# Thirteen tiles of a dense expert table read during a key search, into a buffer of later activations

## The chip, the cores and the metric

The kernel runs on one core of a Trainium2 chip. The core has five engines that this text speaks of: PE (matrix multiplies), DVE (elementwise work and the max/index searches), ACT (activations, casts, evacuation of results), POOL (some elementwise work, and the issue of indirect gathers) and SP (which issues the plain loads and stores). Each works through its own queue in order, and they wait for each other on semaphores. Sixteen DMA engines move data between the main memory and the on-chip memory.

The metric is device time in microseconds. Before the change three runs took 1619.58 to 1623.15 us, with a median of 1620.98 us. A separate execution under the profiler gives the views that this text quotes.

## What is computed

The reference is one hybrid decoder block on 512 tokens of width 1024: three attention branches (a forgetting attention, a sliding window, a cross attention into a memory) are gated, merged and added to `x`, and then comes a product-key expert layer, which is the part that the change touches:

```python
q = (h @ w_q).reshape(B, S, PEER_HEADS, 2, half)
s1 = einsum('bshd,hkd->bshk', q[..., 0, :], keys1)
s2 = einsum('bshd,hkd->bshk', q[..., 1, :], keys2)
v1, i1 = lax.top_k(s1, PEER_TOPK);  v2, i2 = lax.top_k(s2, PEER_TOPK)
cand = (v1[..., :, None] + v2[..., None, :]).reshape(..., PEER_TOPK * PEER_TOPK)
sv, si = lax.top_k(cand, PEER_TOPK)
experts = i1[si // PEER_TOPK] * N_KEYS + i2[si % PEER_TOPK]
gates = softmax(sv)
a = einsum('cd,ced->ce', h, u[experts])
out = einsum('ce,ced->cd', gelu(a) * gates, v[experts])
```

There are 8 heads, 16 chosen experts for each head and token, and 16384 experts, so `u` and `v` are tables of 16384 rows of 1024 floats (64 MiB each).

## The kernel before

The 512 tokens are four blocks of 128. Block 0 goes first through the mixers and its own key search; blocks 1 to 3 follow as one group. For the expert layer the blocks are treated in two ways. Blocks 0 and 1 are gathered: for each of their 128 chosen experts per token a row of `u` and later a row of `v` is fetched by an indirect DMA that POOL issues (L833), and DVE (L843, L852), or ACT and POOL (L848, L849), work it in. Blocks 2 and 3 (`DENSE`) are dense: their activations against all 16384 experts are computed by PE, 128 tiles of 128 experts each, and the gates, which are zero for an expert that wasn't chosen, are multiplied in. A **U tile** is such a tile of the table, transposed on the host (`uT`), 128 x 1024 floats or 512 KB. `dense_u(k)` reads tile k, multiplies it with the dense tokens `h2f` (L971, eight multiplies, which the trace counts as sixteen matmuls) and puts the GELU of the result into `ga(k)` (L973), which is slot k of the tile `soon`. `soon` has 52 slots of 256 floats for each partition; the slots from 52 on are in a tile that is opened later.

The stages around the change, in the order of the program:

- **The second search** (`search(qq, h2T, f, BIG)`, for blocks 1 to 3). For each head SP loads two halves of the query weights `w_pq` into a ring of three buffers `raw` (`load_raw`, L110), ACT rounds them into `whi` (L116), DVE subtracts to get `wlo` (L128), PE multiplies three times (L142 to L144) with the tokens, which stand in the wide tiles `hhi` and `hlo`, ACT copies the result into `qp` (L716), PE makes the scores (L720), ACT copies them into `s` (L723), and DVE finds the sixteen best of each (L678 to L682). The search is a generator which yields an estimated cost after each piece; their running sum is `spent`, about 105 at the end. The loop around it starts a gathered row of block 0 with every 4.6 of cost (`step(apart=True)`: POOL issues the gather, ACT scales the row, POOL adds it), and calls `dense_u` for U tiles 0 to 7 whenever `spent` has passed another 13. Those eight tiles are read by `load_raw`, that is into the same ring of three `raw` buffers as the query weights.
- **The cover stage.** U tiles 8 to 31 go through PE while DVE weighs the gates (`weigh`), works out the chosen experts (`choose`, `numbers_of`) and adds rows of `v` for block 0. From tile 8 on a U tile is read into a ring of six (`URING`), three in `hhi` and three in `hlo`, as soon as the tile six before it is used up; `fetch_u_to` asks for five tiles ahead. `hhi` and `hlo` come free when the search has made its last query product.
- **The spread stage.** DVE builds one-hot sides (L1026), PE multiplies them into gates (L1041), DVE weighs the kept activations (L1044), and U tiles 32 to 56 (`LAG` is 57) go through PE in between.
- **The last stage.** All 128 tiles of `v` go through PE, with the 71 U tiles that are left, whose ring is now the three places of `hhi`.

Up to the end of the search the order of every engine's instructions is worked out by a planner that simulates the program with estimated times; `keep_in_program_order` pins one instruction behind the one that the program issued before it on the same engine. After the search (`tc.manual_schedule`) the orders of PE, DVE and POOL are those of the program, and the planner orders only SP and ACT.

Of the kernel before, what the change touches and what calls it, by code (L numbers as in the profile page):

```python
# [16 lines left out]
S, D, NB, KC = 512, 1024, 4, 8  # L17
# [4 lines left out]
NK = 128  # L22
# [5 lines left out]
ND = len(DENSE)  # L28
TD = 128 * ND
FIRST_U, COVER, DURING, AFTER = 8, 24, 25, 0  # L30
KEPT = FIRST_U + COVER
SPILT = (128 - KEPT) // 3
AMONG, UNWEIGHED = 1.0, 14
LAG = FIRST_U + COVER + DURING + AFTER
GA_LATE = 6
URING, URING_V = 6, 3
# [20 lines left out]
def tile_block(ctx: ExitStack, tc: tile.TileContext, t: dict, out: bass.AP):  # L57
    nc = tc.nc
# [12 lines left out]
    def bank(tag):  # L71
        return psum.tile([128, 512], F32, tag=tag, name=tag, bufs=BANKS[tag])
# [26 lines left out]
    def load_raw(src, n):  # L99
        loads[0] += 1  # L100
        pool = early[0] if early and loads[0] % (RAW_MORE + 3) >= 3 else wp
        raw = pool.tile([128, WSLOT], F32, tag="raw", name="raw")
        fill(raw, src, n)
        return raw

    def fill(raw, src, n):
        if len(src.shape) == 3:
            nc.sync.dma_start(raw[:, :n].rearrange("p (c w) -> p c w", c=src.shape[0]), src.rearrange("c p w -> p c w"))
        else:
            nc.sync.dma_start(raw[:, :n], src)  # L110
# [29 lines left out]
    def mm3(ps, l, r, first=True, last=True):  # L140
        (lh, ll), (rh, rl) = l, r
        PE.matmul(ps, lh, rh, start=first, stop=False)  # L142
        PE.matmul(ps, lh, rl, start=False, stop=False)  # L143
        PE.matmul(ps, ll, rh, start=False, stop=last)  # L144
# [4 lines left out]
    def wide(tag, nb, dt=F32):  # L149

        slot = big.tile([128, (1 if tag == "mg0" else BIG) * D], dt, tag=tag, name=tag)
        return slot[:, :nb * D]

    def by_token(x):
        return x.rearrange("p (b d) -> p b d", d=D)
# [44 lines left out]
    def factors(sums, nb):  # L200

        ss = small_f(BIG, "rss", 2)[:, :nb]
        V.reduce_sum(ss, sums[:, :nb], axis=AX.X)
        return rsqrt_mean(ss, nb, D)

    def diagonals(r, nb):
        dg = small.tile([128, BIG, 128], F32, tag="dg", name="dg", bufs=1)
        for b in range(nb):
            A.activation(dg[:, b], ident, AF.Copy, scale=r[:, b:b + 1])
        return dg  # L210

    def turn(xs, g, hi, lo, dg=None, tags=("tp", "sc")):

        w = 128 * len(xs)
        for dc in range(KC):
            ps = bank(tags[dc % len(tags)])
            for b, x in enumerate(xs):
                dst, src = ps[:, b * 128:(b + 1) * 128], x[:, dc * 128:(dc + 1) * 128]
                if dg is None:
                    PE.transpose(dst, src, ident)  # L220
                else:
                    PE.matmul(dst, src, dg[:, b], start=True, stop=True)
            A.activation(hi[dc], ps[:, :w], AF.Copy, scale=g[:, dc:dc + 1])
            if lo:
                V.scalar_tensor_tensor(lo[dc], ps[:, :w], g[:, dc:dc + 1], hi[dc].bitcast(F32),
                                       op0=OP.mult, op1=OP.subtract)
# [692 lines left out]
    gq, acc, late, v_raw, u_raw = {}, {}, [], {}, {}  # L919
    soon = dp.tile([128, LAG + 1 - GA_LATE, TD], F32, name="ga", bufs=1)  # L920

    def ga(k):
        s = k % (LAG + 1)
        return soon[:, s] if s <= LAG - GA_LATE else late[0][:, s - (LAG + 1 - GA_LATE)]

    def fetch_u(k):
        if not FIRST_U <= k < NK:
            return
        s = (k - FIRST_U) % URING if k < LAG else (k - LAG + 1) % URING_V
        if s % BIG == 0:  # L930
            if k - FIRST_U < URING:
                u_ring[s // BIG] = by_token(wide(("hhi", "hlo")[s // BIG], BIG))
        u_raw[k] = u_ring[s // BIG][:, s % BIG]
        if k > LAG + 2:
            tc.keep_in_program_order(nc.scalar.dma_start(u_raw[k], t["uT"][k]))
        else:
            nc.sync.dma_start(u_raw[k], t["uT"][k])

    u_ring, u_next = [None, None], [FIRST_U]

    def fetch_u_to(k):
        while u_next[0] <= min(k, NK - 1):
            fetch_u(u_next[0])
            u_next[0] += 1

    def split_u(k):
        return k >= LAG and (k - LAG) % U_SPLIT > 0

    def dense_u(k):

        if k < FIRST_U:
            w = load_raw(t["uT"][k], D)[:, :D]
        else:
            fetch_u_to(min(k + URING - 1, LAG + 1) if k < LAG else k)
            w = u_raw.pop(k)
        if split_u(k):
            hi, lo = (gp[0].tile([128, D], F32R, tag=tag, name=tag, bufs=1) for tag in ("uhi", "ulo"))
            A.copy(hi, w)
            yield
            V.tensor_sub(lo, w, hi.bitcast(F32))  # L960
            yield
            ps, hi, lo = bank("mm"), *(x.rearrange("p (n w) -> p n w", n=KC) for x in (hi, lo))
            for dc in range(KC):
                mm3(ps[:, :TD], (hi[:, dc], lo[:, dc]), [x[dc] for x in h2s], dc == 0, dc == KC - 1)
            A.activation(ga(k), ps[:, :TD], AF.Gelu)
            return
        w = w.rearrange("p (n w) -> p n w", n=KC)
        yield
        ps = bank("mm")
        for dc in range(KC):  # L970
            PE.matmul(ps[:, :TD], w[:, dc], h2f[dc], start=dc == 0, stop=dc == KC - 1)  # L971
            yield
        A.activation(ga(k), ps[:, :TD], AF.Gelu)  # L973
# [5 lines left out]
    with tc.tile_pool(name="qb", bufs=2) as qq:  # L979
        turn([x1[b] for b in GROUPS[1]], g2, *h2T)  # L980
        spent, dg, credit[0] = 0.0, None, 0.0
        for cost in search(qq, h2T, f, BIG):
            spent += cost
            if dg is None and spent > 12.0:
                V.tensor_copy(rstd[:, 1:NB], factors(sums, BIG))
                dg = diagonals(rstd[:, 2:NB], ND)
                turn([x1[b] for b in DENSE], g2, h2f, None, dg)
            credit[0] += cost
            while credit[0] >= PER_ROW and NJ <= done[0] < known[0]:
                credit[0] -= PER_ROW  # L990
                with tc.high_priority(-LATER):
                    step(apart=True)
            if k_u < FIRST_U and spent > 104.0 / FIRST_U * (k_u + 1):
                list(dense_u(k_u))
                k_u += 1
# [36 lines left out]
    def spread(n):  # L1032
# [9 lines left out]
        c = t0 % TG  # L1042
        kept = soon[:, :KEPT, i * 128 + t0:i * 128 + t0 + GT]
        V.tensor_mul(kept, ps[:, :, :KEPT].rearrange("p t k -> p k t"), kept)  # L1044
        for hf in range(3):
            k0 = KEPT + hf * SPILT
            A.copy(stage[0][hf][:, :, c:c + GT], ps[:, :, k0:k0 + SPILT].rearrange("p t k -> p k t"))
        if c + GT == TG:
            for hf in range(3):
                k0 = KEPT + hf * SPILT  # L1050
                nc.sync.dma_start(gd[i][:, k0 // GK:(k0 + SPILT) // GK, t0 // TG],
                                  stage[0][hf].rearrange("p (a k) t -> p a (k t)", k=GK))

    def get_gates(k, part):

        k -= k % GK
        if not KEPT <= k < NK or not 0 <= part < GQ_PARTS:
            return
# [52 lines left out]
    while k_u < FIRST_U + COVER:  # L1111
        if k_u == FIRST_U + UNWEIGHED:
            list(weigh(cp, f, 1))
        list(dense_u(k_u))
        k_u += 1
# [19 lines left out]
    for n in range(AHD, NBAT + AHD):  # L1135
        if n < NBAT:
            build_sides(n)
        if n == NBAT - PLAIN_ROWS:
            ahead[0] = AHEAD
        if n == NBAT - V_EARLY:  # L1140
            for k in range(VFAR):
                fetch_v(k)
        credit[0] += STEPS_N
        while credit[0] >= 1.0 and done[0] < known[0]:
            credit[0] -= 1.0
            step()
        if (n + 4) % PER == 0 and n + 4 < NBAT:
            turn_block((n + 4) // PER)
        spread(n - AHD)
        for _ in range(STEPS_U):  # L1150
            if tile_u is None and FIRST_U + COVER + n * DURING // NBAT >= k_u:
                tile_u = dense_u(k_u)
                next(tile_u)
                k_u += 1
            elif tile_u is not None and next(tile_u, 1):
                tile_u = None
# [132 lines left out]
```

## Time and profile before

| | |
|---|---|
| median of three runs | 1620.98 us |
| profiled execution | 1613.45 us, of which its span from first to last instruction is 1611.6 us |
| DVE busy in the span | 1406.2 us (87%) |
| ACT busy, POOL busy | 782.9 us (49%), 780.6 us (48%) |
| first matmul of a U tile | 689.6 us from the start of the span |
| first matmul of U tile 8 | 771 us |
| first one-hot side of the spread stage | 857.4 us |
| moved by the DMA engines | 531.85 MB, mean 330 GB/s |

Times inside the profile are microseconds from the start of the span. In a timeline a row is a start, a duration, the engine, the line of the kernel and the operation, then what is written and read; several alike are merged (x16), and square brackets give the idle time of the engine before the row and what ended it. In the list of waits a row says who waited for whom, and the three numbers are the total in microseconds, the number of times, and the longest. In the windows table every engine has its busy time in the window, then come the granted TensorE clock, the mean share of the DMA engines that were busy, and GB/s. Busy times of merged rows can overlap by a little, since an instruction may start before the one before it has fully ended.

### The profile page before, as it was taken

What the parts mean: (1) busy time and instruction counts of PE and PEld (TensorE: products, weight loads), DVE (VectorE), ACT (ScalarE), POOL (GpSimd) and SP (SyncE); (2) the same over time, 40 slices, a digit from 0 to 9 for tenths busy, and PEclk for the clock granted to TensorE, in tenths of its full rate; (3) what the DMA queues carried; (4) which work ended last, traced back from release to release, by engine and by line L of the source; (5) the groups of instructions that cost most, each with busy time, mean ns of one, the idle gap of its engine ahead of it and who ended that gap; (6) DMA issues with size and microseconds to landing.
All of it is one profiled execution on the core that took longest, in us unless ns stands there. A gap on an engine that the chain in (4) does not pass through costs nothing.

```text
span 1611.6 us, 26380 instructions
## 1 busy us (share of the span) xinstructions
PE 1532.9 (95%) x9030; PEld 1377.0 (85%) x9030; DVE 1406.2 (87%) x2721; ACT 782.9 (49%) x1782; POOL 780.6 (48%) x625
## 2 busy tenths in 40 slices
PE   5999999998998999998999999899999999999998
PEld 5999899988887989987888999688888888888887
DVE  5677458889888999999999999889899999999997
ACT  6787437645445443553116888344344343433432
POOL 1100011767566455588664333556655566555551
PEclk9999999999998999999999999999999999999999
DMA  8586753899998899967898999999999999999995
GB/s 300 176 283 223 236 196 118 285 358 310 326 344 287 280 360 342 326 203 264 320 404 304 367 385 350 379 394 394 399 409 407 395 411 408 410 412 409 406 407 215
DMA packets 180406, 531.85 MB, mean 330 GB/s; under 512 B 17456, under 2 KB 46384, under 8 KB 180272
## 3 DMA queue, kind: packets, MB, share of 16 engines
q0 software_dynamic: 73728, 268.47, 44.6%
q1 hardware_dynamic: 96752, 226.04, 38.6%
q10 hardware_dynamic: 9792, 35.66, 5.6%
q8 instruction: 71, 1.16, 0.3%
q14 instruction: 63, 0.52, 0.1%
HBM read 515.42 MB, written 14.68 MB: 329 GB/s over the span
## 4 chain that ended last, share of the span: by engine, by line
PE 36%; DVE 22%; DMA 17%; issue 15%; POOL 7%; ACT 2%; SPq 0%; DVEq 0%; POOLq 0%; ACTq 0%
DMA row<-in_peer_u_dram,eidx 8%; DMA row<-in_peer_v_dram,eidx 7%; POOL row L833 6%; PE mm L143 6%; PE mm L144 6%; PE mm L142 6%; DVE mg L852 6%; DVE o L1026 3%; DVE scr L843 3%; PE mm L971 3%; DVE wlo L128 2%; PE mm L295 2%; PE sc L142 1%; PE sc L143 1%; PE sc L144 1%
## 5 line engine op out<-in xcount | busy, mean ns | idle before, releaser
L833 POOL DMA_INDIRECT row<-in_peer_v_dram,eidx x256 | 346.0, 1351 | 269.2 <-DVE mg L852 150.0
L833 POOL DMA_INDIRECT row<-in_peer_u_dram,eidx x256 | 330.9, 1292 | 271.6 <-DVE scr L843 161.8
L843 DVE SCALAR_TENSOR_TENSOR scr<-row,own 128x1024 bf16<-128x1024 f32 x256 | 314.5, 1228 | 31.7 <-DMA row<-in_peer_u_dram,eidx 29.6
L128 DVE TENSOR_TENSOR wlo<-raw,whi 128x1024 fp32r<-128x1024 f32 (+1 forms) x243 | 305.6, 1259 | 36.3 <-ACT whi L116 35.7
L852 DVE SCALAR_TENSOR_TENSOR mg<-row,acts,mg 128x1024 f32<-128x1024 f32 x237 | 304.4, 1285 | 20.5 <-DMA row<-in_peer_v_dram,eidx 18.2
L971 PE MATMUL mm<-h2f,hhi 128*128 128x256 f32 x976 | 223.2, 379 | 1.6 <-ACT ga L973 1.6
L971 PEld LDWEIGHTS mm<-h2f,hhi 128*128 128x128 f32 x976 | 182.5, 190 | 26.6 <-ACT ga L973 2.0
L116 ACT CAST whi<-raw 128x1024 fp32r<-128x1024 f32 (+1 forms) x148 | 155.0, 1050 | 90.2 <-PE mm L143 47.1
L189 POOL TENSOR_TENSOR rsy<-rsv,mhalf 128x4 f32<-128x4 f32 (+5 forms) x25 | 38.8, 1553 | 219.8 <-DVE rsv L188 126.3
L1089 ACT CAST ah<-ga 128x256 fp32r<-128x256 f32 x116 | 47.0, 407 | 150.8 <-PE tp L143 118.1
L1091 ACT CAST whi<-raw 128x1024 fp32r<-128x1024 f32 x96 | 100.4, 1046 | 39.6 <-PE tp L144 26.0
L142 PE MATMUL mm<-hhi,whi 128*128 128x384 f32 x320 | 110.8, 347 | 5.9 <-ACT ga L973 4.6
L143 PE MATMUL mm<-hlo,whi 128*128 128x384 f32 x320 | 111.2, 347 | 0.0
L144 PE MATMUL mm<-hhi,wlo 128*128 128x384 f32 x320 | 110.1, 344 | 0.0
L142 PE MATMUL mm<-whi,hhi 128*128 128x256 f32 (+1 forms) x360 | 104.6, 292 | 3.0 <-DVE g L572 1.9
L142 PE MATMUL sc<-whi,ah 128*128 128x512 f32 x256 | 107.3, 419 | 0.0
L143 PE MATMUL sc<-wlo,ah 128*128 128x512 f32 x256 | 101.1, 395 | 3.4 <-DVE wlo L128 3.4
L143 PE MATMUL mm<-wlo,hhi 128*128 128x256 f32 (+1 forms) x360 | 103.1, 287 | 0.2 <-DVE wlo L128 0.2
L144 PE MATMUL mm<-whi,hlo 128*128 128x256 f32 (+1 forms) x360 | 101.7, 284 | 0.0
L973 ACT ACTIVATE ga<-mm 128x256 f32<-128x256 f32 x84 | 31.7, 379 | 143.5 <-PE mm L971 143.4
L144 PE MATMUL sc<-whi,al 128*128 128x512 f32 x256 | 101.1, 395 | 0.0
L142 PE MATMUL tp<-whi,ah 128*128 128x512 f32 x256 | 100.6, 393 | 0.0
(289 smaller groups left out, 3941.8 us busy)
## 6 DMA issues: line engine op xcount, KB each, us to landing
raw<-in_peer_v_dram SPq DMA_DIRECT2D x96, 512.0 KB, 8.1
hhi<-in_uT_dram ACTq DMA_DIRECT2D x68, 512.0 KB, 7.7
raw<-in_w_tr_dram SPq DMA_DIRECT2D x48, 512.0 KB, 5.0
raw<-in_w_nat_dram SPq DMA_DIRECT2D x40, 512.0 KB, 5.7
last<-in_peer_v_dram SPq DMA_DIRECT2D x32, 512.0 KB, 7.4
hhi<-in_uT_dram SPq DMA_DIRECT2D x28, 512.0 KB, 6.7
raw<-in_w_o_dram SPq DMA_DIRECT2D x24, 512.0 KB, 6.1
hlo<-in_uT_dram SPq DMA_DIRECT2D x24, 512.0 KB, 7.2
```

Of the source, the lines that this page charges most:

```text
L116: A.copy(hi[:, :n * w], raw[:, :n * w])
L128: V.tensor_sub(lo, raw, hi.bitcast(F32))
L142: PE.matmul(ps, lh, rh, start=first, stop=False)
L143: PE.matmul(ps, lh, rl, start=False, stop=False)
L144: PE.matmul(ps, ll, rh, start=False, stop=last)
L833: G.indirect_dma_start(out=r, out_offset=None, in_=t["peer_" + tab], in_offset=bass.IndirectOffsetOnAxis(ap=eidx[b][:, j:j + 1], axis=0))
L843: V.scalar_tensor_tensor(scr, r, 1.0, h2n[b], op0=OP.mult, op1=OP.mult, accum_out=acts[b][:, c]))
L852: V.scalar_tensor_tensor(x1[b], r, acts[b][:, c], x1[b], op0=OP.mult, op1=OP.add))
L971: PE.matmul(ps[:, :TD], w[:, dc], h2f[dc], start=dc == 0, stop=dc == KC - 1)
L1026: V.tensor_tensor(o, numbers[:, None, None, :].to_broadcast([128, 2, GT, NK]), eT[:, :2, ts, None].to_broadcast([128, 2, GT, NK]), op=OP.i ...
L1089: A.copy(ah, a)
L1091: A.copy(hi, raw)
```

## The change

U tiles 0 to 12 (`PRE_U`) are read into `soon`: tile k goes into slots 4k to 4k+3, which have its size, so 13 tiles fill the 52 slots. The activation of a tile is written to slot k when that tile has been multiplied, and slot k belongs to tile k // 4, which has been used by then. The reads are issued by SP in the loop around the second search, tile k as soon as `spent` is over 6 k, each pinned behind the SP instruction that the program issued before it. Tiles 0 to 7 no longer use `load_raw`. `dense_u` is called at the same places as before; for tiles 0 to 7 it asks for no reads. The ring in `hhi` and `hlo` begins with tile 13, which together with 14 to 18 is asked for at `dense_u(8)`. The place of a tile in the ring is counted from 13 on, and the last tile that is asked for in the spread stage is 57, where it was 58.

```diff
+PRE_U = 13
...
     def fetch_u(k):
-        if not FIRST_U <= k < NK:
+        if k < PRE_U:
+            u_raw[k] = soon[:, 4 * k:4 * k + 4].rearrange("p a b -> p (a b)")
+            tc.keep_in_program_order(nc.sync.dma_start(u_raw[k], t["uT"][k]))
             return
-        s = (k - FIRST_U) % URING if k < LAG else (k - LAG + 1) % URING_V
+        s = (k - PRE_U) % URING if k < LAG else (k - LAG + 1 + (LAG - 1 - PRE_U) % URING) % URING_V
         if s % BIG == 0:
-            if k - FIRST_U < URING:
+            if k - PRE_U < URING:
                 u_ring[s // BIG] = by_token(wide(("hhi", "hlo")[s // BIG], BIG))
         u_raw[k] = u_ring[s // BIG][:, s % BIG]
...
-    u_ring, u_next = [None, None], [FIRST_U]
+    u_ring, u_next = [None, None], [0]
...
     def dense_u(k):
 
-        if k < FIRST_U:
-            w = load_raw(t["uT"][k], D)[:, :D]
-        else:
-            fetch_u_to(min(k + URING - 1, LAG + 1) if k < LAG else k)
-            w = u_raw.pop(k)
+        if k >= FIRST_U:
+            fetch_u_to(min(max(k, PRE_U) + URING - 1, LAG) if k < LAG else k)
+        w = u_raw.pop(k)
...
+            while u_next[0] < PRE_U and spent > 6.0 * u_next[0]:
+                fetch_u_to(u_next[0])
             credit[0] += cost
```

## The prediction, on record before the result

> **What bounds the kernel now.** I read the table of windows first, one window for each stage, then the waits and the timelines of the two stages that the change touches.
>
> ```profile
> span 1611.6 us, 26380 instructions
> ...
> core 0: us, PE busy (x) PEld busy (x) DVE busy (x) ACT busy (x) POOL busy (x), PEclk, DMA share, GB/s
> 645.00:690.00 45.00, 43.53 (x263) 42.72 (x262) 44.61 (x112) 22.27 (x38) 25.00 (x25) 0.96 0.88 315
> 690.00:735.00 45.00, 40.34 (x224) 38.21 (x224) 44.91 (x253) 23.51 (x34) 34.44 (x32) 0.96 0.64 212
> 735.00:771.00 36.00, 31.55 (x166) 28.20 (x166) 33.15 (x250) 10.64 (x18) 33.16 (x31) 1.00 0.73 261
> 771.00:856.00 85.00, 83.36 (x387) 73.05 (x386) 80.69 (x131) 12.64 (x29) 50.49 (x39) 1.00 0.97 374
> 856.00:1000.00 144.00, 141.35 (x897) 131.01 (x896) 143.81 (x202) 120.15 (x468) 48.78 (x48) 1.00 0.99 352
> ...
> 1040.00:1594.00 554.00, 542.91 (x2771) 465.35 (x2770) 509.14 (x672) 218.16 (x337) 314.79 (x213) 1.00 1.02 402
> ```
>
> The search (the first three windows) is DVE's: in 126 us it is idle for 0.39 + 0.09 + 2.85 = 3.3 us, while PE is idle for 10.6 us. The cover stage (771 to 856) is a tie: PE idles 1.6 of 85 us, DVE 4.3. The spread stage is DVE's (0.2 us idle of 144). Only in the last stage are the DMA engines full (1.02, 402 GB/s) with PE next to them (98%).
>
> So the question is what a U tile that comes earlier can do for DVE in the search, and whether PE's tie in the cover stage is worth anything. The search's small idle times are seen in the timelines of DVE, ACT and PE:
>
> ```profile
> 750.61 0.68 DVE L678 MAX8 v<-s 128x8 f32<-128x128 f32 x3 [1.24 <-ACT s L723]
> ...
> 760.00 0.68 DVE L678 MAX8 v<-s 128x8 f32<-128x128 f32 x3 [1.57 <-ACT s L723]
> ...
> 729.07 1.05 ACT L116 CAST whi<-raw 128x1024 fp32r<-128x1024 f32 x1 [4.23 <-DMA raw<-in_w_pq_dram]
> ...
> 758.07 1.15 ACT L848 ACTIVATE row<-row,acts 128x1024 f32<-128x1024 f32 x1 [4.79 <-DMA row<-in_peer_v_dram,eidx]
> ...
> 759.49 0.48 ACT L723 COPY s<-sc 128x384 f32<-128x384 f32 x1
> ...
> 754.10 3.62 PE L971 MATMUL mm<-h2f,raw 128*128 128x256 f32 x16
> 759.64 0.94 PE L720 MATMUL sc<-keys,qp 128*128 128x128 f32 x6 [1.92 <-ACT qp L716]
> 760.41 7.07 PE L971 MATMUL mm<-h2f,raw 128*128 128x256 f32 x32
> 767.68 3.69 PE L971 MATMUL mm<-h2f,raw 128*128 128x256 f32 x16 [0.19 <-DMA raw<-in_uT_dram]
> 771.21 3.62 PE L971 MATMUL mm<-h2f,hhi 128*128 128x256 f32 x16
> ```
>
> DVE stalls twice, 1.24 and 1.57 us, for the copied scores of the last heads. The second copy stands in ACT's queue behind a row of `v` for which ACT had waited 4.79 us. No U tile holds PE up but the last, by 0.19 us, and then PE goes from tile 7 straight on to tile 8 at 771.21. There is no gap at the end of the search that an earlier read could close, since the ring's first reads had been issued 19 us before:
>
> ```profile
> 752.40 0.33 SPq L937 DMA_DIRECT2D hlo<-in_uT_dram  x1
> 752.78 1.68 SPq L937 DMA_DIRECT2D hhi<-in_uT_dram  x3
> ```
>
> Then the end of the cover stage, DVE and PE:
>
> ```profile
> 854.87 2.59 DVE L852 SCALAR_TENSOR_TENSOR mg<-row,acts,mg 128x1024 f32<-128x1024 f32 x2
> 857.38 4.61 DVE L1026 TENSOR_TENSOR o<-tg,eT 128x1024 f32<-128x1024 f32 x4
> ...
> 856.00 0.38 PE L1013 MATMUL acc<-cst,e 128*128 128x128 f32 x2
> 859.13 1.32 PE L1041 MATMUL sc<-o 128*128 128x128 f32 x8 [2.65 <-issue]
> ```
>
> DVE goes from the last rows (until 857.46) to the one-hot sides without a gap. PE is through with tile 31 at about 856 and then stands still for 2.65 us until the first sides are there. A PE that comes earlier to this point waits longer.
>
> **The change part by part.**
>
> *Reads of tiles 0 to 12.* SP issues 13 loads in the search where it issued 8, and six ring loads at its end as before (now 13 to 18, not 8 to 13). DVE's first look at a score, and the first and the last of the five U reads that SP's timeline had before 735 (two of them before 690):
>
> ```profile
> L678 DVE MAX8 v<-s x48: 266/276/296, 662.3 to 762.6; 128x8 f32<-128x128 f32 x48
> ...
> 668.34 0.33 SPq L110 DMA_DIRECT2D raw<-in_uT_dram  x1
> ...
> 732.36 0.33 SPq L110 DMA_DIRECT2D raw<-in_uT_dram  x1
> ```
>
> From 662 to 771 are 109 us for 8 x (6 x 1.6 + 3 x 1.2) = 105.6 of cost, so tile k is asked for at about 662 + 6.2 k: five reads by 690 and seven from 690 to 735. A read is 512 KB, 0.524 MB. That is 3 x 0.524 = 1.6 MB more in the first window, 35 GB/s on 315, and 4 x 0.524 = 2.1 MB more in the second, 47 GB/s on 212. Both sums, 350 and 259, stay under the 402 of the last stage. I cost it at nothing; what covers it is the idle share of the DMA engines (0.12 and 0.36 of those windows). If that cover is gone, the gathered rows come late, and ACT and DVE wait for them (the slow cases below).
>
> The Trainium skill (DMA: Bandwidth & Descriptors, Specifications) gives a limit of about 358 GB/s of main memory for each core. This trace doesn't agree: 402 GB/s over 554 us. By that limit the first window would be full, and 350 of 358 would leave the gathers no room.
>
> *The ring of `raw`.* Eight loads leave it, and the query weights have three buffers to themselves. The list of waits of the search shows what they cost:
>
> ```profile
> ACT row L848 <- DMA row<-in_peer_v_dram,eidx: 20.6, 9, 5.9
> ACT whi L116 <- DMA raw<-in_w_pq_dram: 9.1, 3, 4.2
> ...
> DVE v L678 <- ACT s L723: 2.8, 2, 1.6
> ```
>
> ACT waits 9.1 us for late query weights, the longest 4.23 us ahead of 729.07; from there the last heads' product, scores and copies follow. These waits should mostly go. What DVE gets of it is bounded by its two stalls: between 0 (the copies stand behind gathered rows, 20.6 us of waits that the change doesn't touch) and 1.24 + 1.57 = 2.8 us. I take 2.8, because 4.2 us earlier weights are more than either stall; 0 stays for the range.
>
> *Tiles 8 to 12 ready on chip.* They remove nothing that the trace shows: PE had tile 8 without a wait. Five reads (2.6 MB, at 402 GB/s 6.5 us of the DMA engines) leave the cover stage, whose DMA share is 0.97. Who waited there?
>
> ```profile
> DVE gden L754 <- ACT ex L750: 2.5, 1, 2.5
> ...
> PE mm L971 <- ACT ga L973: 1.6, 1, 1.6
> ```
>
> Neither waits for a transfer; both are the softmax's turn on ACT. So 0.
>
> *PE.* If the tiles fill its idle 10.6 us of the search, it reaches tile 8 earlier by a few us, and waits them away at 859.13. So 0. The other end: if DVE came earlier too, PE would have to as well, and this is where its lead would be used.
>
> *The orders.* DVE, ACT, PE and SP are planned anew for the whole search. One cost there depends on the order:
>
> ```profile
> L128 DVE TENSOR_TENSOR wlo<-raw,whi x14: 1204/1220/3078, 648.0 to 738.8; 128x1024 fp32r<-128x1024 f32 x14
> ...
> 680.97 1.23 DVE L128 TENSOR_TENSOR wlo<-raw,whi 128x1024 fp32r<-128x1024 f32 x1
> 685.19 2.98 DVE L128 TENSOR_TENSOR wlo<-raw,whi 128x1024 fp32r<-128x1024 f32 x1 [0.35 <-ACT whi L116]
> ...
> L849 POOL TENSOR_TENSOR mg<-mg,row x19: 2352/2377/2649, 684.6 to 769.1; 128x1024 f32<-128x1024 f32 x19
> ...
> L128 DVE TENSOR_TENSOR wlo<-raw,whi 128x1024 fp32r<-128x1024 f32 x14 | 24.9, 1778 | 0.4 <-ACT whi L116 0.4
> ```
>
> Fourteen subtractions take 24.9 us where 14 x 1.22 would be 17.1: some are stretched to as much as 3.08 us, and those fall in the time in which POOL adds rows. That is 7.8 us on DVE's path. Earlier weights would move subtractions ahead of POOL's adds (these begin at 684.6) or off them; another order may also hit more of them. Ends: 7.8 gained, and as much lost; I take 0, since the number of both operations stays and POOL is hardly moved.
>
> The Trainium skill (SBUF — State Buffer, "SBUF: two separate sides") states why: DVE, with two inputs in SBUF, and GpSimd share a port pair that is locked for a whole instruction, and the loser waits. The trace agrees: 3.08 is less than 1.22 + 2.38.
>
> *Tile 58.* It is asked for when the last stage begins, not in the spread stage:
>
> ```profile
> 979.79 0.33 SPq L937 DMA_DIRECT2D hhi<-in_uT_dram  x1
> ...
> 1002.53 0.35 SPq L937 DMA_DIRECT2D hhi<-in_uT_dram  x1
> ```
>
> The first row was tile 58, the second 59. At worst 0.524 MB more stand in the full last stage, 0.524 / 402 GB/s = 1.3 us; at best its place is free (tile 55 is done) before 1000 and it costs nothing. I take half, 0.6.
>
> **Sum**: -2.8 + 0.6 = -2.2 us. On the profiled span 1611.6 becomes 1609.4, and its execution of 1613.45 us becomes 1611.2. The median of the runs is 7.5 us above that execution; I put the same difference on the median: 1620.98 - 2.2 = **1618.8 us**, 0.14% faster. Runs of this kernel tell about 0.2%, 3.2 us, from no change, so this is "the same".
>
> **The rivals.**
>
> *Faster, 1615.* The earlier weights take the subtractions off POOL's adds. If half of the 7.8 us goes, that is -3.9 more: 1614.9; all of it, 1611. For it speaks that the first seven subtractions, until 680.97, had 1.2 us each, ahead of POOL's first add. Against it: weights are used in the order of the heads, and `s` has room for three heads only, so few can be drawn that far ahead.
>
> *Slower, 1625 to 1628.* A U tile on PE goes ahead of the last heads' scores. Before, tiles 5 to 7 ran behind the last score product (760.41, 767.68), the last of them for want of its data. With data some 30 us earlier the planner may put one or two of them into what it takes for idle time of PE. It decides when a tile starts before the product at 759.64: DVE has no work left there (1.57 us idle), so each such tile is 3.5 us (7.07 for two) on DVE's path. One: 1620.98 + 3.5 + 0.6 = 1625.1; two: 1628.6. For it: tile 4 already stands at 754.10, between the scores. Against it: the scores come first in the program.
>
> *Slower by the transfers, 1625.* If the first window had no room, three more reads would delay gathers by 3 x 0.524 / 358 GB/s = 4.4 us. This is the page's limit, which the 402 GB/s speak against.
>
> *It doesn't do what it says, 1621.* The reads are pinned on SP behind the weight loads that the program issued before; where these wait for a buffer, a tile comes hardly earlier than now. Then nothing changes.
>
> **How the numbers follow.** Forecast 0.42; faster 0.33; slower by PE's order 0.16; slower by the transfers 0.04; not done 0.05. The forecast's own range (0 to 2.8 gained, 0 to 1.3 lost) is 1618.2 to 1622.3. Faster by over 0.2%: 0.33. Same: 0.42 + 0.05 = 0.47. Slower: 0.20. The range takes in the faster case to twice its half (to 1613) and the slower one nearly to two tiles: 1613 to 1627.
>
> **What would show it.** Right: ACT's 9.1 us for `w_pq` gone; DVE's two stalls gone; DVE's end of the search (the first `ex`, L747) some 3 us earlier, and the first `o` (L1026) earlier by the same; PE's wait ahead of the first L1041 longer. Wrong: the mean of L128 in the search well under or over 1778 ns; U tiles of PE ahead of the last L720 with DVE waiting for `s`; rows that DVE waits for between 645 and 690; or a difference that arises only after 1000, which no term here but tile 58 explains.

## The result: 0.5% faster, and the profile after

Six runs of the changed kernel took 1610.36 to 1616.01 us, median 1612.02, beside a median of 1620.95 us of the kernel before: a ratio of 0.9947, 95% interval 0.9930 to 0.9965, or some 8.9 us. The forecast was 1618.8 us, with "the same" as the likeliest outcome and a range from 1613 to 1627; the time lies just below the range.

Lines of the kernel after stand one to three further down than before (L128 is L129, L720 is L721, L971 is L972, L1026 is L1029, L1041 is L1044). The table of windows of the kernel after, in the same three windows of the search and in the cover stage:

```profile
core 0: us, PE busy (x) PEld busy (x) DVE busy (x) ACT busy (x) POOL busy (x), PEclk, DMA share, GB/s
645.00:690.00 45.00, 42.62 (x264) 41.72 (x265) 44.36 (x110) 20.31 (x37) 26.16 (x25) 1.00 1.01 389
690.00:735.00 45.00, 41.81 (x242) 39.95 (x241) 45.00 (x291) 26.43 (x37) 40.60 (x36) 0.99 0.72 247
735.00:771.00 36.00, 33.21 (x165) 29.38 (x163) 32.19 (x219) 12.29 (x21) 30.85 (x28) 0.97 0.64 224
771.00:856.00 85.00, 80.90 (x378) 71.14 (x378) 83.27 (x131) 12.39 (x32) 52.12 (x38) 1.00 0.93 351
```

The DMA engines are full in the first window (share 1.01, 389 GB/s; before 0.88 and 315), and DVE is as busy as before in the first two. The last two windows are of little use for a comparison, since the stages' ends have moved; for that the following marks are better. From the list of waits of the search, after:

```profile
ACT row L849 <- DMA row<-in_peer_v_dram,eidx: 20.5, 8, 4.4
...
DVE v L679 <- ACT s L724: 0.8, 1, 0.8
```

ACT's 9.1 us of waits for query weights are gone from the list, DVE's waits for copied scores went from 2.8 to 0.8 us, and ACT's waits for gathered rows are what they were. The subtraction in the lines of DVE, after:

```profile
L129 DVE TENSOR_TENSOR wlo<-raw,whi 128x1024 fp32r<-128x1024 f32 x14 | 22.4, 1603 | 0.6 <-ACT whi L117 0.6
```

It takes 22.4 us where it took 24.9. The first `ex` came at 767.8 us instead of 771.7, and the first one-hot side at 853.4 instead of 857.4. That is 4 us of some 9, and the two profiled spans differ by 1.5 us only (1610.1 and 1611.6). So the first question was what the profiled execution of before had that the usual one hasn't.

### The profile page after: what moved, and what is told of

Read it like the earlier page. It is cut to its first block, busy times and chain, and to the rows that moved or that the text cites. A ratio compares the mean times of both kernels' runs of the same rounds, so it can differ in the third digit from the quotient of the medians.

```text
span 1610.1 us, 26369 instructions
## 1 busy us (share of the span) xinstructions
PE 1530.4 (95%) x9030; PEld 1374.5 (85%) x9030; DVE 1402.8 (87%) x2721; ACT 783.1 (49%) x1782; POOL 792.0 (49%) x625
## 4 chain that ended last, share of the span: by engine, by line
PE 32%; DVE 22%; DMA 19%; issue 15%; POOL 8%; ACT 3%; SPq 0%; POOLq 0%; DVEq 0%; ACTq 0%
DMA row<-in_peer_v_dram,eidx 11%; POOL row L834 8%; DMA row<-in_peer_u_dram,eidx 7%; PE mm L144 6%; PE mm L145 5%; PE mm L143 5%; DVE mg L853 5%; DVE o L1029 3%; DVE wlo L129 3%; DVE scr L844 2%; PE mm L296 2%; PE mm L972 2%; ACT o L1032 1%; PE sc L143 1%; PE sc L145 1%
## 5 line engine op out<-in xcount | busy, mean ns | idle before, releaser
L834 POOL DMA_INDIRECT row<-in_peer_v_dram,eidx x256 | 350.0, 1367 | 266.8 <-DVE mg L853 151.6
L834 POOL DMA_INDIRECT row<-in_peer_u_dram,eidx x256 | 335.9, 1312 | 268.1 <-DVE scr L844 145.1
L129 DVE TENSOR_TENSOR wlo<-raw,whi 128x1024 fp32r<-128x1024 f32 (+1 forms) x243 | 302.8, 1248 | 35.5 <-ACT whi L117 34.3
L853 DVE SCALAR_TENSOR_TENSOR mg<-row,acts,mg 128x1024 f32<-128x1024 f32 x237 | 303.2, 1279 | 21.8 <-DMA row<-in_peer_v_dram,eidx 16.5
L972 PE MATMUL mm<-h2f,hhi 128*128 128x256 f32 x944 | 216.0, 379 | 0.0
L972 PEld LDWEIGHTS mm<-h2f,hhi 128*128 128x128 f32 x944 | 176.7, 190 | 24.0
```

The lines of the kernel that those rows point to most:

```text
L129: V.tensor_sub(lo, raw, hi.bitcast(F32))
L834: G.indirect_dma_start(out=r, out_offset=None, in_=t["peer_" + tab], in_offset=bass.IndirectOffsetOnAxis(ap=eidx[b][:, j:j + 1], axis=0))
L853: V.scalar_tensor_tensor(x1[b], r, acts[b][:, c], x1[b], op0=OP.mult, op1=OP.add))
```

## The experiments

**Theory 1**: there are two gains, both because U tiles no longer share the three `raw` buffers with the query weights. The search gets shorter, and so does the cover stage. **Rival A**: it is the five tiles 8 to 12, which leave the full cover stage. **Rival B**: early reads as such, which let PE use its idle times in the search. **Rival C**: nothing but luck of the orders, above all in the last stage.

### The same two programs again

No edit. Kernel before:

> The kernel before, again, to see how far two executions of one program differ and where. The profiled execution was 1613.45 us, the six timed ones 1617.5 to 1623.2. Theory 1 (the gain lies in the search): the first softmax operation of the second search (ex) stands near 771.7 us again, and what makes the usual execution 7 us longer is spread over the stages or lies in the last one. Theory 2 (the profiled execution was a lucky one in the last stage): from the first split of h2f (about 1006) to the end it takes about 612 us, not 605.5.

Kernel after:

> The changed kernel, again. Ratio 0.993 to 0.9965 once more. Theory 1: ex near 767.8 us, the spread stage's first one-hot side near 853.4, and from the first split of h2f to the end 608 us as in the first profile. Theory 2: its last stage is some 4 us shorter than that of the kernel before in executions of the same day.

Measured: the kernel before against itself 0.9992 (0.9975 to 1.0009); the kernel after 0.9939 (0.9925 to 0.9952). The second profile of before has a span of 1618.3 us and a search as long as in the first. The timelines of PE, SP and DVE in it:

```profile
764.77 7.07 PE L971 MATMUL mm<-h2f,raw 128*128 128x256 f32 x32
775.44 5.38 PE L971 MATMUL mm<-h2f,raw 128*128 128x256 f32 x16 [3.60 <-DMA raw<-in_uT_dram]
780.65 10.52 PE L971 MATMUL mm<-h2f,hhi 128*128 128x256 f32 x48
...
760.00 0.33 SPq L937 DMA_DIRECT2D hlo<-in_uT_dram  x1
760.38 1.37 SPq L937 DMA_DIRECT2D hhi<-in_uT_dram  x3
761.79 0.98 SPq L937 DMA_DIRECT2D hlo<-in_uT_dram  x2
764.29 0.33 SPq L110 DMA_DIRECT2D raw<-in_uT_dram  x1
...
864.62 4.62 DVE L1026 TENSOR_TENSOR o<-tg,eT 128x1024 f32<-128x1024 f32 x4 [3.89 <-ACT eT L1015]
```

The last SP row is tile 7. It has to wait until tile 4 has left its `raw` buffer, and by then the six reads of the ring (3.1 MB) stand ahead of it. It lands some 11 us after its issue; PE waits 3.60 us for it, in order, ahead of tiles 8 to 31; and at the other end of the cover stage DVE waits 3.89 us for PE's transposes (through ACT's copy `eT`). The read in the first profile had been late too, by 0.19 us. Theory 2 of the expectations, a lucky last stage, fell: from the first split of `h2f` to the end of the span it took 605.5 us in the first profile and 604.9 in the second. In the kernel after it took 608.0 and then 605.7 us, so the second didn't repeat the 608 of its expectation either.

### One half of the change alone

Tiles 0 to 7 early, 8 to 13 in the ring as before:

```diff
-PRE_U = 13
+PRE_U = 8
```

> The change with PRE_U = 8: tiles 0 to 7 go into the later activations' buffer early, tiles 8 to 13 into the ring as before. Theory 1 (the weights have the ring of raw to themselves, which moves the search): ex near 768, ratio 0.994 to 0.997, as with the whole change. Rival (the five tiles 8 to 12 that leave the cover stage do it): ex near 771.7 or the time within 0.2% of the kernel before.

Tiles 0 to 7 through `raw` as before, only 8 to 12 early:

```diff
+        if k < FIRST_U:
+            return
         if k < PRE_U:
...
-    u_ring, u_next = [None, None], [0]
+    u_ring, u_next = [None, None], [FIRST_U]
...
-        w = u_raw.pop(k)
+        w = u_raw.pop(k) if k >= FIRST_U else load_raw(t["uT"][k], D)[:, :D]
```

> Tiles 0 to 7 through the ring of raw as before, only tiles 8 to 12 read early into the later activations' buffer. Theory 1: ex near 771.7, ratio 0.998 to 1.002. Rival (tiles 8 to 12): ratio 0.994 to 0.997, and ACT's 9 us of waits for query weights stay.

Measured: 0.9944 (0.9924 to 0.9965) for tiles 0 to 7 alone, which is the whole gain, and 1.0027 (1.0006 to 1.0048), slower than before, for tiles 8 to 12 alone. With tiles 0 to 7 alone the first `ex` came at 772.0 us, not near 768, but there the search also began some 3 us later (665.9 against 662.8); its length, 106.1 us, is what theory 1 meant. Rival A fell, since tiles 8 to 12 alone bring no gain; that they cost something was expected by neither side. Why this kernel is slower is in its waits of the search and its lines of DVE:

```profile
ACT row L849 <- DMA row<-in_peer_v_dram,eidx: 25.3, 11, 10.3
ACT whi L117 <- DMA raw<-in_w_pq_dram: 16.5, 4, 8.8
...
L129 DVE TENSOR_TENSOR wlo<-raw,whi 128x1024 fp32r<-128x1024 f32 x15 | 31.8, 2122 | 1.4 <-ACT whi L117 1.3
```

ACT waits 16.5 us for query weights (before 9.1), and fifteen subtractions take 31.8 us, 13.5 more than 15 x 1.22. The cause that the changed kernel removes is there in a larger size, and the search is 5.6 us longer.

### Tile 7 alone, and a ring of their own

The cover stage's term by itself: only tile 7 is read early.

```diff
-            w = load_raw(t["uT"][k], D)[:, :D]
+            w = load_raw(t["uT"][k], D)[:, :D] if k < 7 else u_raw.pop(7)
...
+            if 7 not in u_raw and k_u < 7 and spent > 60.0:
+                u_raw[7] = soon[:, 28:32].rearrange("p a b -> p (a b)")
+                tc.keep_in_program_order(nc.sync.dma_start(u_raw[7], t["uT"][7]))
             credit[0] += cost
```

> The kernel before, with tile 7 alone read early (at spent 60) into slots 28 to 31 of the later activations' buffer; tiles 0 to 6 through the ring of raw. Theory 1 (two separate gains: the search is some 4.5 us shorter because the query weights have the ring of raw to themselves, and the cover stage is some 4 us shorter because tile 7 no longer comes behind the six ring reads): the cover stage, from the first ex to the first one-hot side, takes 85.7 us, not 89.7; the search stays near 109.4; ratio 0.9970 to 0.9985. Rival (what shortens the cover stage is that the search ends early, or that tiles 8 to 12 are there): the cover stage stays at 89.7 in this run, ratio 0.999 to 1.001.

The search's term by itself: tiles 0 to 7 are read where the kernel before reads them, but into three places of their own.

```diff
-            w = load_raw(t["uT"][k], D)[:, :D]
+            w = soon[:, 40 + 4 * (k % 3):44 + 4 * (k % 3)].rearrange("p a b -> p (a b)")
+            nc.sync.dma_start(w, t["uT"][k])
```

> The kernel before, with tiles 0 to 7 read where dense_u asks for them, but into a ring of three places of their own in the later activations' buffer (slots 40 to 51). The query weights have the ring of raw to themselves; tile 7 must wait until tile 4 has been used, as before. Theory 1: ACT's waits for query weights (9 to 10 us) go, the search takes 105 us instead of 109.4, the cover stage stays near 89.7 if tile 7 stands behind the ring reads on SP again; ratio 0.996 to 0.998. Rival (the search is shorter since the tiles come early, so that PE has them in its idle times): the search stays at 109; ratio 0.999 to 1.001.

Measured: tile 7 alone 0.9994 (0.9982 to 1.0006), the ring of their own 0.9966 (0.9953 to 0.9979). With tile 7 early the cover stage does take 85.6 us, as theory 1 had it, but its ratio is not the 0.997 to 0.9985 that was expected. In PE's and DVE's timeline it is seen why:

```profile
759.14 0.94 PE L720 MATMUL sc<-keys,qp 128*128 128x128 f32 x6 [3.84 <-ACT qp L716]
759.91 8.76 PE L971 MATMUL mm<-h2f,raw 128*128 128x256 f32 x32
768.51 3.62 PE L971 MATMUL mm<-h2f,ga 128*128 128x256 f32 x16
```

```profile
DVE v L678 <- ACT s L723: 4.7, 2, 3.6
```

PE has tile 7 without a wait, but DVE waits 4.7 us for the last scores, and the search is 1.3 us longer: one stall taken for another. In the ring of their own tile 7 waits for tile 4's place as before, and it is read behind the ring's six again; yet it is on time, since tile 4 is done at 754 and not at 758 or 764. That part of theory 1, that its cover stage would stay at 89.7, was wrong: here the cover stage's gain came although tile 7 was read behind the six. The search took 107.6 us, about halfway between the 105 of theory 1 and the 109 of the rival. Nor does this run hold every read where it was: the three places are free at the start, and tiles 0 to 2 were issued at 645 to 646 us (before at 668, 682 and 708). So it separates the ring from the early reading only in part.

### How early

```diff
-            while u_next[0] < PRE_U and spent > 6.0 * u_next[0]:
+            while u_next[0] < PRE_U and spent > 8.0 * u_next[0]:
```

> The change with one read for every 8 of cost instead of 6, so the last of the thirteen at 96 of 105. Theory 1: the same as the change, ratio 0.993 to 0.996, search 105, cover stage 85.7. Rival (the early reads, 389 GB/s at a DMA share of 1.01 in the first window, cost something): 1 to 3 us faster than the change.

And with 4.0 in that place:

> The change with one read for every 4 of cost instead of 6, so the last of the thirteen at 48 of 105. One for every 8 gave 0.9971, one for every 6 gave 0.9939 and 0.9947. If earlier is better: 0.992 to 0.994. If the pace only shuffles the planner's orders (theory 1): anywhere between 0.993 and 0.998. If the full DMA engines of the first window cost gathers: slower than the change by 1 to 4 us, with DVE waiting for rows before 690.

Measured: 0.9971 (0.9955 to 0.9988) with 8, 0.9999 (0.9982 to 1.0017) with 4. Both miss what was expected: with 8 the ratio is just above 0.993 to 0.996 and the kernel not faster than the change, and with 4 it is above every range that was named, though DVE waited for no row before 690. With 4 the whole gain is gone, although no tile is late and ACT's waits for weights are 2.5 us in all. ACT's and DVE's timeline in it:

```profile
760.84 1.15 ACT L849 ACTIVATE row<-row,acts 128x1024 f32<-128x1024 f32 x1 [8.54 <-DMA row<-in_peer_v_dram,eidx]
761.90 0.36 ACT L974 ACTIVATE ga<-mm 128x256 f32<-128x256 f32 x1
762.16 0.47 ACT L724 COPY s<-sc 128x384 f32<-128x384 f32 x1
...
762.66 0.68 DVE L679 MAX8 v<-s 128x8 f32<-128x128 f32 x3 [6.95 <-ACT s L724]
```

The last scores wait on ACT behind the scaling of a gathered row that ACT had waited 8.54 us for, and DVE waits 6.95 us for them. All thirteen early reads had been issued by 690. In the kernel after a row stands ahead of the last scores on ACT too; what differs is how late that row is. Its gather was issued 0.97 us ahead of the first of the ring's six reads there (748.74 and 749.71) and landed after 4.9 us; with 4 it was issued 2.0 us behind that read (751.37 and 749.35) and took 9.4 us. In the other traces the same gather took 4.1 to 4.4 us where it was issued 3 us or more ahead of the six reads, 5.9 us at 0.3 us ahead, and 7.2 to 8.5 us from 0.1 us ahead to 1.1 us behind. So the lateness goes with the six reads, but no run moved the gather or the reads alone. So rival B fell in its simple form: earlier is not better. That the pace acts through the planner's orders (rival C, within the search), by which of the gather and the reads is issued first, is what the traces suggest; no run tells it apart.

### More executions of before, of tile 7 and of after

No edit.

> The kernel before, a third execution under the profiler, to see how often tile 7 is late. Theory 1 (PE waits for tile 7 behind the ring reads, and DVE then waits for PE at the first one-hot side; the first profile, in which PE waited 0.19 us, was the rare one): PE waits 2 to 4 us for tile 7, DVE some 4 us at the first one-hot side, the cover stage takes 88 to 90 us. Rival: the cover stage takes 85.7 us in most executions, and the usual 7 us over the first profile lie elsewhere.

> As the run before it: a fourth execution of the kernel before. Theory 1: cover stage 88 to 90 us. Rival: 85.7 us.

> The kernel with tile 7 alone read early, a second execution under the profiler. Theory 1: the cover stage takes 85.7 us again and PE has no wait for tile 7; its search is not shorter than that of the kernel before (109 to 111 us). Rival: its cover stage is as long as that of the kernel before in the same call.

> The changed kernel, a third execution under the profiler. Search near 105 us, cover stage 85.7 us, no wait of PE for tile 7. Open is what comes after the first one-hot side: 756.7 and 758.9 us to the end in the two traces so far, 753.7 to 757.4 in four of the kernel before. If the change costs something in the last stage (tile 58 among it), it is 757 or more again; if the two were chance, 754 to 756.

Measured from the traces of all executions, in us. "Search" is from DVE's first look at a score to `ex`, "cover" from there to the first one-hot side. "Stretch" is the time of all subtractions `wlo` in the search over 1.22 us each. "DVE idle" is DVE's wait for the scores and, in the search's end, for POOL's candidates. "Tile 7" is PE's wait for it.

| execution | search | stretch | DVE idle | tile 7 | cover | search + cover |
|---|---|---|---|---|---|---|
| before, first | 109.4 | 7.8 | 2.8 | 0.2 | 85.7 | 195.1 |
| before, second | 109.4 | 8.3 | 2.1 | 3.6 | 89.7 | 199.1 |
| before, third | 109.4 | 8.4 | 2.0 | 3.3 | 88.5 | 197.9 |
| before, fourth | 109.0 | 8.1 | 1.7 | 3.1 | 88.1 | 197.1 |
| after, first | 105.0 | 5.3 | 1.2 | 0 | 85.6 | 190.6 |
| after, second | 104.8 | 5.4 | 1.1 | 0 | 85.7 | 190.5 |
| after, third | 104.8 | 5.4 | 1.1 | 0 | 85.6 | 190.4 |
| tiles 0 to 7 alone | 106.1 | 4.6 | 3.1 | 0 | 85.7 | 191.8 |
| ring of their own | 107.6 | 4.4 | 3.8 | 0 | 85.6 | 193.2 |
| pace 8 | 105.5 | 3.0 | 4.4 | 0 | 85.7 | 191.2 |
| pace 4 | 111.3 | 3.4 | 8.5 | 0 | 86.0 | 197.3 |
| tile 7 alone, first | 110.7 | 7.2 | 4.7 | 0 | 85.6 | 196.3 |
| tile 7 alone, second | 111.3 | 7.1 | 5.2 | 0 | 85.6 | 196.9 |
| tiles 8 to 12 alone | 115.0 | 13.5 | 1.6 | 3.8 | 89.8 | 204.8 |

Two things are to be read here. The search's length is 98.7 us plus stretch plus DVE's idle time, to within 1.2 us in every row: DVE has a fixed amount of work there, and only these two terms differ. And PE waits 3 us or more for tile 7 in three of four executions of before; where it does, the cover stage takes 2.4 to 4.0 us more. Over the kernels the last column follows the timed runs: 190.4 to 193.2 us go with ratios of 0.994 to 0.997, 196.3 to 197.3 with 0.999 to 1.000, and 204.8 with 1.003.

The mean of before is 197.3 us, that of after 190.5: 6.8 us of the 8.9 measured are in these two stages, 4.4 in the search (2.8 of it less stretch, 1.0 less idle, 0.4 less waiting of DVE for `whi`) and 2.4 in the cover stage. The rest is open. From the first one-hot side to the end it took 753.7 to 757.4 us in the four traces of before and 756.7, 758.9 and 755.8 us in the three of after: 1.6 us more on the mean, within what executions of one program differ by. The third trace, 755.8, lies where the last expectation had put chance (754 to 756); a cost of the change in the later stages isn't shown. So the whole spans differ by 5.2 us on the mean of the traces (1615.6 and 1610.4), the timed runs by 8.9; a handful of traced executions doesn't tell where the other 3 to 4 us are. Part of it is which executions were traced: the four of before took 1617.4 us on the mean, less than the median of the timed runs beside any of the experiments (1619.5 to 1621.0).

## Why the prediction was wrong

Two terms that the forecast put at nothing failed: the end of the search, which was worth 2.4 us in the cover stage, and the orders, worth 2.8 us (means of the traces). Against them stands a term that was put too high, the ring of `raw`, with 1.0 of its 2.8 us. In these two stages 6.8 us were gained where the forecast had 2.8. Some 2 us of the measured 8.9 have no place in the traces, so it stays open how much of the miss is theirs.

**What bounds.** That DVE sets the search held, more exactly than it was put. That the cover stage is a tie held too, but the step "There is no gap at the end of the search that an earlier read could close" failed. It rested on one execution, in which PE waited 0.19 us for tile 7. The row itself was the warning: a wait of 0.19 us says that a transfer landed *just* too late, and that PE, in a tie with DVE, had no slack to take it. In three other executions the same wait was 3.1 to 3.6 us, and DVE paid for it with 2.0 to 3.9 us at the first one-hot side. The forecast also put the profiled difference on the median, though that execution was 7.5 us under the median; this very stall is 2.4 to 4.0 us of it. The longer wait of PE ahead of the first gates, which the forecast named as a sign, didn't come: 2.65 us before, 2.58 to 2.71 after, since DVE came earlier too.

**The range.** Its lower end doesn't follow from its own words. Twice the half of the faster rival is all of it, which the prediction puts at 1611, and not 1613. The measured 1612.02 lies between the two.

**Tiles 8 to 12: 0.** Right: without them the time is the same (0.9944 against 0.9947 and 0.9939).

**The ring of `raw`: 2.8.** The mechanism was right: ACT's waits for weights went, and DVE's stalls with them, but for 0.4 to 0.8 us. DVE's idle time fell by 1.0 us, not 2.8, on the mean of the traces, since the other executions of before had smaller stalls to begin with (1.0 to 2.1 us for the scores), and POOL's candidates came late by 0.3 to 0.7 us after (by 0.7 and 0.8 in two of the four of before).

**The orders: 0 of 7.8.** Mis-sized: 2.8 us were gained, and as much or more in every kernel in which the weights had the ring to themselves (3.0 to 5.4 us of stretch left, against 7.1 to 8.4 with U tiles in the ring, and 13.5 where the weights came later still). It is the mechanism of the faster rival. Not as put there, though: the subtractions were not drawn ahead of POOL's first add. From 685 on they meet fewer of its adds: in each trace of before five subtractions are stretched, in each of after four, and each of them overlaps one running add and ends 1.1 us after it. Why they meet fewer isn't shown: the pace alone moved the stretch between 3.0 and 5.4 us, so it hangs on when each of the two starts, and no run moved a subtraction alone. What the Trainium skill (SBUF — State Buffer, "SBUF: two separate sides") says of the locked port pair fits this: no subtraction waited for more than one add. The Trainium skill gives the pair to whichever starts first; by the start times of the profile that holds only from a lead of some 0.7 us on. With tiles 8 to 12 alone a subtraction took 4.01 us, since it began 0.54 us ahead of the add and yet let it go first; in the kernel after one that began 0.68 us ahead went first, and the add took 2.80 us. The timelines of DVE and POOL, two rows of each of these kernels:

```profile
727.61 4.01 DVE L129 TENSOR_TENSOR wlo<-raw,whi 128x1024 fp32r<-128x1024 f32 x1
728.15 2.38 POOL L850 TENSOR_TENSOR mg<-mg,row 128x1024 f32<-128x1024 f32 x1
...
709.32 1.22 DVE L129 TENSOR_TENSOR wlo<-raw,whi 128x1024 fp32r<-128x1024 f32 x1
710.00 2.80 POOL L850 TENSOR_TENSOR mg<-mg,row 128x1024 f32<-128x1024 f32 x1
```

**The reads.** Nine were issued by 690, not five: they follow SP's order and not DVE's progress, and the first two were issued at 649.8 and 650.4, ahead of DVE's first look at a score at 662.8. They filled the DMA engines (1.01, not 0.88 plus a little), and still DVE waited for no row before 690. The rival of a full main memory didn't come; 389 GB/s in that window is again above the 358 that the Trainium skill (DMA: Bandwidth & Descriptors, Specifications) gives.

**Slower by PE's order.** Of tiles 5 to 12 none stood ahead of the last scores in the kernel after. They follow them, with one wait of 2.43 us, as PE's timeline of it shows:

```profile
755.30 0.94 PE L721 MATMUL sc<-keys,qp 128*128 128x128 f32 x6 [1.32 <-ACT qp L717]
756.07 13.98 PE L972 MATMUL mm<-h2f,ga 128*128 128x256 f32 x64
772.48 14.08 PE L972 MATMUL mm<-h2f,ga 128*128 128x256 f32 x64 [2.43 <-ACT ga L974]
786.40 10.52 PE L972 MATMUL mm<-h2f,hhi 128*128 128x256 f32 x48
```

The late scores that the experiments did have came from rows on ACT, not from tiles on PE.

**Tile 58: 0.6.** It was asked for at 992 us, not 980, with 59 within 7 us of it. Whether this cost anything is below what the runs tell apart; it wasn't tried by itself.

## What to carry to other kernels

When buffers of a small ring are shared by two streams with different consumers, the slower consumer can set when the other stream's loads start; giving each stream its own places was worth more here (0.9966) than reading one tile earlier (0.9994). A wait near zero for a transfer, on an engine that has no slack later, can be a stall of several us in other executions, as it was here in three of four: profile a kernel more than once before a stall is costed at nothing. And where a planner orders the queues, a small change of a read's place can make a wait longer that stands ahead of work on the path; time more than one setting.

## What the runs showed of the hardware that was not expected

A 512 KB read that stood behind six others of its size in SP's queue landed about 11 us after its issue (764.29 to 775.4), where the median of the same reads was 4.4 us in the first profile of before. A subtraction on DVE that began up to 0.54 us ahead of an add on POOL waited for the whole add and ended 1.1 us after it; one that began 0.67 us or more ahead went first, and the add took 2.6 to 2.8 us and not 2.4. That holds for every overlap of the two in the traces of the search. And the profiled executions of one program moved a stage of 86 us by up to 4 us, with PE's granted clock at 0.983 to 0.987 in all of them.
